# Column mean of 8192x8192: row groups added by VectorE into an accumulator instead of summed one by one by TensorE

## The chip, the cores and the metric

The kernel runs on one core of a Trainium2 chip; the other cores are idle. The metric is the device time of one execution in microseconds (us), as a median over repeated executions. Ratios of two kernels are computed as the mean time of one kernel's runs over that of the other's runs of the same rounds, so they are not quite the ratio of the medians that are quoted beside them. With one core there is one clock to look at: its mean granted value in the profiles is 0.765 before.

## The reference

```python
x = randn(8192, 8192).astype(float32)      # 268.4 MB
out = np.mean(x, axis=0)                    # 8192 numbers
```

Every input number is read once and added once. There is nothing to reuse.

## The kernel before

Rows are taken in groups of 128, one row per partition ("row group"). A group is 4 MiB, a load brings two. TensorE sums over the 128 partitions with a matmul whose weights are all 1/8192, 32 columns wide; four such matmuls sit side by side in the array (the trace shows them overlap: after 613 us a group of four starts every 0.86 us, though it is eight instructions of 0.59 us), and all row groups accumulate in PSUM.

```python
    J = 2
    ld = ctx.enter_context(tc.tile_pool(name="ld", bufs=3))        # 3 x 64 KB per partition
    ...
    for ti in range(n_t - 1):                                       # 31 loads of 8 MiB
        t = ld.tile([P, J, N], f32)
        nc.sync.dma_start(out=t[:], in_=xt[ti])
        for j in range(J):
            sums(t, j, range(NBLK + 1), ti == 0 and j == 0, False)  # 15 matmuls of 512 columns, 4 of 128
    ...                                                             # last 8 MiB in four column pieces:
    cuts = [(0, 8), (8, 12), (12, 15), (15, 16)]                    # blocks of 512 columns
    for lo, hi in cuts:
        for j in range(J):
            sums(t, j, range(lo, hi), False, j == J - 1)
        ...                                                         # VectorE copies the bank, ACT queue sends it
```

## Time and profile before

| | before |
|---|---|
| time, median of 3 | 634.08 us (633.62 to 634.26) |
| span in the profile | 632.0 us |
| load queue, share of 16 DMA engines | 98.4% |
| TensorE (PE) busy | 304.2 us, 48% |
| VectorE (DVE) busy | 3.0 us |

"Busy" is time under instructions of that engine; the shares of different engines overlap. The prediction below shows the lines that say what bounds the kernel. Two more views are needed later. The first is the list of groups of instructions (name, shapes, count, then busy us and mean ns of one, then idle time before them and its cause):

```profile
L47 PE MATMUL bank<-t,ones 128*32 128x512 f32 x1920 | 297.0, 739 | 324.2 <-DMA t<-in_x_dram 324.2
L47 PE MATMUL edge<-t,ones 128*32 128x128 f32 x512 | 51.5, 279 | 0.0
```

The kernel has 1,216 matmuls, but the profile counts 2,432: each fp32 matmul is two instructions here, and each comes with a weight load (2,432 of those too). The second view is the list of transfer queues (packets, megabytes, share of the 16 engines' time):

```profile
q1 hardware_dynamic: 5552, 268.44, 98.4%
q8 instruction: 19, 0.31, 0.2%
q10 hardware_dynamic: 38, 0.03, 0.0%
```

A packet is a piece of a transfer that one DMA engine moves: of the first row's, 3,968 carry 64 KB each in 2.42 us, and 16 at a time at that pace make 433 GB/s, which is the stream's rate. The first row is the loads, the last the results.

### The profile page before, as it was taken

Reading aid. Unit: us, or ns where it says so; the run is one execution under the profiler, and the core shown is the slowest. Engines: PE = TensorE matmul, PEld = TensorE weight load, DVE = VectorE, ACT = ScalarE, POOL = GpSimd, SP = SyncE. Lnnn points to the kernel's source line nnn. Section 1 sums busy time; section 2 is a strip of 40 time slices with the busy share of each in tenths; the row PEclk is TensorE's granted clock in tenths of the full one; section 3 lists DMA queues with packets and bytes.
Section 4 is the critical chain, followed back from the end, with each engine's and each line's share of the span. In section 5 each row is a group of like instructions: output and inputs, shape, how many; then the busy total and the mean of one; then the engine's idle time right before and its main releaser. Section 6 shows DMA issues by size and latency. Waiting matters only on the chain.

```text
span 632.0 us, 4990 instructions
## 1 busy us (share of the span) xinstructions
PE 304.2 (48%) x2432; PEld 99.9 (16%) x2432; DVE 3.0 (0%) x6; POOL 0.2 (0%) x4
## 2 busy tenths in 40 slices
PE   0542555434654345554365534466433655344555
PEld 0210111111211111110111111122101211011111
DVE  0000000000000000000000000000000000000001
POOL 0000000000000000000000000000000000000000
PEclk9977876778776788767777667886678776678769
DMA  9999999999999999999999999999999999999994
GB/s 398 427 437 456 399 465 408 452 411 449 416 444 419 441 444 416 457 402 465 403 456 428 431 428 436 424 448 412 452 423 441 432 431 428 436 431 428 437 401 199
DMA packets 5609, 268.78 MB, mean 425 GB/s; under 512 B 579, under 2 KB 583, under 8 KB 1110
## 3 DMA queue, kind: packets, MB, share of 16 engines
q1 hardware_dynamic: 5552, 268.44, 98.4%
q8 instruction: 19, 0.31, 0.2%
q10 hardware_dynamic: 38, 0.03, 0.0%
HBM read 268.44 MB, written 0.03 MB: 425 GB/s over the span
## 4 chain that ended last, share of the span: by engine, by line
DMA 80%; PE 17%; another core or an unknown queue 2%; SPq 0%; issue 0%; DVE 0%; DVEq 0%
DMA t<-in_x_dram 80%; PE bank L47 15%; PE edge L47 2%; SPq L75 0%; DVE r L83 0%; DVEq L116 0%
## 5 line engine op out<-in xcount | busy, mean ns | idle before, releaser
L47 PE MATMUL bank<-t,ones 128*32 128x512 f32 x1920 | 297.0, 739 | 324.2 <-DMA t<-in_x_dram 324.2
L47 PEld LDWEIGHTS bank<-t,ones 128*32 128x32 f32 x1920 | 85.9, 132 | 489.8 <-DMA t<-in_x_dram 311.7
L47 PE MATMUL edge<-t,ones 128*32 128x128 f32 x512 | 51.5, 279 | 0.0
L47 PEld LDWEIGHTS edge<-t,ones 128*32 128x32 f32 x512 | 23.9, 111 | 38.5 <-issue 38.5
L83 DVE COPY r<-bank 128x512 f32<-128x512 f32 (+1 forms) x4 | 2.8, 690 | 625.1 <-PE bank L47 625.1
L88 DVE COPY redge<-edge 128x128 f32<-128x128 f32 x1 | 0.3, 277 | 0.0
L105 POOL MEMSET const-bfloat16-1.0<- 128x1 bf16 x1 | 0.1, 101 | 0.0
L105 POOL MEMSET const-uint8-127<- 128x1 uint8 x1 | 0.1, 101 | 0.0
L105 POOL MEMSET const-float32-0.0<- 128x1 f32 x1 | 0.1, 98 | 0.2 <-issue 0.2
L105 POOL MEMSET const-float32-1.0<- 128x1 f32 x1 | 0.1, 98 | 0.0
L42 DVE MEMSET ones<- 128x32 f32 x1 | 0.1, 85 | 0.8 <-PEq L105 0.8
## 6 DMA issues: line engine op xcount, KB each, us to landing
t<-in_x_dram SPq DMA_DIRECT2D x1, 4096.0 KB
t<-in_x_dram SPq DMA_DIRECT2D x1, 2048.0 KB, 45.1
t<-in_x_dram SPq DMA_DIRECT2D x1, 1536.0 KB, 48.1
t<-in_x_dram SPq DMA_DIRECT2D x1, 512.0 KB, 39.2
t<-in_x_dram SPq DMA_DIRECT2D x31, 49.0
out_dram<-r ACTq DMA_DIRECT2D x3, 8.0 KB
out_dram<-r ACTq DMA_DIRECT2D x1, 6.0 KB
out_dram<-redge ACTq DMA_DIRECT2D x1, 2.0 KB
```

The costliest lines, as they stand in the source:

```text
L42: nc.vector.memset(ones[:], 1.0 / M)
L47: nc.tensor.matmul(out=dst[32 * q:32 * q + 32, :], lhsT=ones[:], rhs=rhs, start=first, stop=last, tile_position=(0, 32 * q), skip_group_ch ...
L83: nc.vector.tensor_copy(out=r[:32 * n, :], in_=banks[b][:32 * n, :])
L88: nc.vector.tensor_copy(out=r[:], in_=edge[:])
L105: nc = _bacc.Bacc("TRN2", target_bir_lowering=False, num_devices=1)
```

## The change

The intent is to take the arithmetic off TensorE: VectorE adds whole rows into an accumulator of 128x8192, and TensorE only sums over the partitions at the end, for the accumulator and the last two row groups. The accumulator takes 32 KB per partition, so the ring of buffers shrinks from three of 64 KB to two of 64 KB and one of 32 KB. Copies of the results move from VectorE to ACT (ScalarE), except the last small one (`edge`): it stays on VectorE, and its transfer is issued by SP (SyncE) in place of ACT.

```diff
-    ld = ctx.enter_context(tc.tile_pool(name="ld", bufs=3))
+    pairs = ctx.enter_context(tc.tile_pool(name="pairs", bufs=2))
+    singles = ctx.enter_context(tc.tile_pool(name="singles", bufs=1))
+    acc = sg.tile([P, N], f32, name="acc")
 ... (loads go pair, pair, single, pair, pair, single, ...)
-        for j in range(J):
-            sums(t, j, range(NBLK + 1), ti == 0 and j == 0, False)
+        for row in rows:
+            if g == 0:
+                prev = row
+            elif g == 1:
+                nc.vector.tensor_add(out=acc[:], in0=prev, in1=row)
+            elif g < G - 3:
+                nc.vector.tensor_add(out=acc[:], in0=acc[:], in1=row)
+            else:                                   # group 61, in four quarters
+                for c in range(0, N, 4 * F):
+                    s = slice(c, c + 4 * F)
+                    nc.vector.tensor_add(out=acc[:, s], in0=acc[:, s], in1=row[:, s])
 ... (group 62 is loaded whole, group 63 in four column pieces)
+    sums(t[:, 0, :], range(NBLK + 1), True, False)  # group 62
+    for b in range(4):
+        sums(acc, range(4 * b, 4 * b + 4), False, False)
     for lo, hi in cuts:
-        for j in range(J):
-            sums(t, j, range(lo, hi), False, j == J - 1)
+        sums(t[:, 1, :], range(lo, hi), False, True)
 ...
-                nc.vector.tensor_copy(out=r[:32 * n, :], in_=banks[b][:32 * n, :])
+                nc.scalar.copy(out=r[:32 * n, :], in_=banks[b][:32 * n, :])
```

More of the change, by code (lines that the diff above doesn't have):

```diff
@@ L29 @@
     F = 512
-    J = 2
+    W = F // 4
     NBLK = N // F - 1
-    W = F // 4
-    n_t = M // (P * J)
-    xt = x.rearrange("(t p j) c -> t p j c", p=P, j=J)
-    ld = ctx.enter_context(tc.tile_pool(name="ld", bufs=3))
+    G = M // P
+    pairs = ctx.enter_context(tc.tile_pool(name="pairs", bufs=2))
+    singles = ctx.enter_context(tc.tile_pool(name="singles", bufs=1))
     sg = ctx.enter_context(tc.tile_pool(name="sg", bufs=1))
@@ L39 @@
     resp = ctx.enter_context(tc.tile_pool(name="res", bufs=1))
-    ones = sg.tile([P, 32], f32)
-    nc.vector.memset(ones[:], 1.0 / M)
+    acc = sg.tile([P, N], f32, name="acc")
+    ones = sg.tile([P, 32], f32, name="ones")
+    warm = sg.tile([P, 32], f32, name="warm")
+    nc.gpsimd.memset(ones[:], 1.0 / M)
+    nc.scalar.copy(out=warm[:], in_=ones[:])
     banks = [psp.tile([P, F], f32, name=f"bank{b}") for b in range(4)]
@@ L55, in mm, with sums @@
         )
-    def sums(t, j, blocks, first, last):
+    def sums(row, blocks, first, last):
         for i in blocks:
             if i < NBLK:
-                mm(banks[i // 4], i % 4, t[:, j, i * F:(i + 1) * F], first, last)
+                mm(banks[i // 4], i % 4, row[:, i * F:(i + 1) * F], first, last)
             else:
@@ L63, in sums @@
                     c = i * F + q * W
-                    mm(edge, q, t[:, j, c:c + W], first, last)
-    for ti in range(n_t - 1):
-        t = ld.tile([P, J, N], f32)
-        nc.sync.dma_start(out=t[:], in_=xt[ti])
-        for j in range(J):
-            sums(t, j, range(NBLK + 1), ti == 0 and j == 0, False)
-    t = ld.tile([P, J, N], f32)
+                    mm(edge, q, row[:, c:c + W], first, last)
+    g = 0
+    k = 0
+    prev = None
+    while g < G - 2:
+        n = 1 if k % 3 == 2 and g + 2 < G - 2 else 2
+        if n == 2:
+            t = pairs.tile([P, 2, N], f32, name="pair")
+            src = x[g * P:(g + 2) * P, :].rearrange("(p j) c -> p j c", j=2)
+            nc.sync.dma_start(out=t[:], in_=src)
+            rows = [t[:, 0, :], t[:, 1, :]]
+        else:
+            t = singles.tile([P, N], f32, name="single")
+            nc.sync.dma_start(out=t[:], in_=x[g * P:(g + 1) * P, :])
+            rows = [t[:]]
+        for row in rows:
[5 more added lines that the diff above has]
+                nc.vector.tensor_add(out=acc[:], in0=acc[:], in1=row)
+            else:
+                for c in range(0, N, 4 * F):
+                    s = slice(c, c + 4 * F)
+                    nc.vector.tensor_add(out=acc[:, s], in0=acc[:, s], in1=row[:, s])
+            g += 1
+        k += 1
+    t = pairs.tile([P, 2, N], f32, name="pair")
+    nc.sync.dma_start(out=t[:, 0, :], in_=x[g * P:(g + 1) * P, :])
     cuts = [(0, 8), (8, 12), (12, 15), (15, 16)]
     for lo, hi in cuts:
-        nc.sync.dma_start(out=t[:, :, lo * F:hi * F], in_=xt[n_t - 1, :, :, lo * F:hi * F])
+        cs = slice(lo * F, hi * F)
+        nc.sync.dma_start(out=t[:, 1, cs], in_=x[(g + 1) * P:(g + 2) * P, cs])
+    sums(t[:, 0, :], range(NBLK + 1), True, False)
+    for b in range(4):
+        sums(acc, range(4 * b, 4 * b + 4), False, False)
     for lo, hi in cuts:
-        for j in range(J):
-            sums(t, j, range(lo, hi), False, j == J - 1)
+        sums(t[:, 1, :], range(lo, hi), False, True)
         if hi <= NBLK:
@@ L89 @@
             o = out[lo * F:hi * F].rearrange("(q c) -> q c", q=4)
-            nc.scalar.dma_start(out=o, in_=r[0:P:32, :])
+            nc.sync.dma_start(out=o, in_=r[0:P:32, :])
 _INS = ['x']
```

## The prediction

> **What bounds the kernel now.** I read the page of the kernel before from the top: busy shares, slices, queues, chain.
>
> ```profile
> span 632.0 us, 4990 instructions
> PE 304.2 (48%) x2432; PEld 99.9 (16%) x2432; DVE 3.0 (0%) x6; POOL 0.2 (0%) x4
> DMA  9999999999999999999999999999999999999994
> q1 hardware_dynamic: 5552, 268.44, 98.4%
> DMA 80%; PE 17%; another core or an unknown queue 2%; SPq 0%; issue 0%; DVE 0%; DVEq 0%
> ```
>
> PE is busy for half of the span, the load queue for 98.4% of it, and the row of DMA slices has one digit below 9, the last. The chain of waits gives PE 17%, which misleads: it follows PE only to the moment when a buffer comes free. Whether that free buffer was urgent is told by the waits of the queue that issues the loads, and by the issues' time to landing:
>
> ```profile
> SPq L68 <- DMA t<-in_x_dram: 275.3, 28, 20.4
> SPq L68 <- PE edge L47: 270.8, 28, 10.5
> t<-in_x_dram SPq DMA_DIRECT2D x31, 49.0
> ```
>
> Per 8 MiB load the issuer waits 9.8 us for an old load and then 9.7 us for PE to finish that buffer; the new load lands 49.0 us after issue. Carrying 8.39 MB alone takes 19.5 us, so a load stands some 29.5 us behind others in the queue: the PE wait is covered three times over. The windows view says that the transfers themselves are at their pace:
>
> ```profile
> core 0: us, PE busy (x) PEld busy (x) DVE busy (x) POOL busy (x), PEclk, DMA share, GB/s
> 120.00:220.00 100.00, 48.76 (x392) 16.08 (x396) 0.00 (x0) 0.00 (x0) 0.76 1.00 434
> 220.00:320.00 100.00, 50.40 (x396) 16.30 (x391) 0.00 (x0) 0.00 (x0) 0.74 1.00 434
> 420.00:520.00 100.00, 50.63 (x406) 16.47 (x398) 0.00 (x0) 0.00 (x0) 0.74 1.00 433
> ```
>
> All 16 engines are taken all the time (share 1.00) at 433 GB/s. So the time is a head of 2 us, a stream of 268.44 MB, and a tail after the last load. Only the stream's rate, a hole in it, or the tail can change the time.
>
> [...]
>
> **The change part by part.** *Removed:* 62 of 64 row groups from PE. It sat beside the stream, so this is worth nothing by itself.
>
> *Added:* 60 VectorE adds of 128x8192 and four of 128x2048. [...] the sum is 60 x 8.69 + 9.2 = 531 us. One row of 4.19 MB takes 4.19/0.4305 = 9.75 us of the stream, using the mean of mid-run and last-part rates. So VectorE needs 89% of the pace: it becomes the second busiest, not the bound.
>
> *The ring:* 160 KB in place of 192 (the accumulator takes 32), and a pair is held for two adds, 17.4 us, instead of PE's 9.7. Call the buffers A (two rows), B (two), S (one) and let A land at 0. B lands at 19.5, S at 29.3, and A's next load should start then. A is free at 17.5, so 12 us early. B is added from 19.5 to 36.9, and its next load starts at 48.8: again 12 us early. S is added from 36.9 to 45.6, and is wanted at 68.3. An issue costs about 2 us before data (the first load took 21.8 us against 19.5 for its bytes), so the queue never runs dry. Issue to landing should fall from 49 to about 32 us.
>
> *Transfers:* 13 row groups now come in 32 KB runs instead of 64, but the last group cut into small pieces is 4 MiB instead of 8. From the slices near the end, where 8 KB runs moved at about 418 GB/s against 433, I estimate 10 ns lost per run and engine: +0.5 us for the singles, -0.3 for the tail. The stream stays within half a microsecond.
>
> *Head:* pool memset and the ACT warm-up copy run during the first load. 0.
>
> *Tail:* here the change shows. The kernel before ends so:
>
> ```profile
> 607.62 5.15 PE L47 MATMUL bank<-t,ones 128*32 128x512 f32 x27 [10.56 <-DMA t<-in_x_dram]
> 617.41 3.64 PE L47 MATMUL bank<-t,ones 128*32 128x512 f32 x32 [0.34 <-DMA t<-in_x_dram]
> 626.06 1.49 PE L47 MATMUL bank<-t,ones 128*32 128x512 f32 x9 [1.73 <-DMA t<-in_x_dram]
> 628.64 0.28 DVE L88 COPY redge<-edge 128x128 f32<-128x128 f32 x1
> 620.99 8.51 ACTq L85 DMA_DIRECT2D out_dram<-r  x4
> 629.59 0.55 ACTq L90 DMA_DIRECT2D out_dram<-redge  x1
> ```
>
> The next-to-last 8 MiB landed at 607.6; PE was done 21.0 us later, the span 24.4 us later. Weight-load starts in the same view show four 512-column blocks side by side ("a quad") in 0.86 us at full clock and 1.7 at half.
>
> Count the changed kernel from the landing of the last pair that VectorE adds (time 0). The row after it lands at 9.8; the last row's pieces at 14.8, 17.3, 19.1, 19.7. The accumulator's quarters are ready at 8.8 + 2.3k: 11.1, 13.4, 15.7, 18.0. PE starts at 9.9 [...] two quads at 1.7, the rest faster, edge 0.3: done at 15.8. It then has accumulator quarters 1 to 3 (until 18.4), the last one with its edge (19.6), and only then the last row, though most of it has landed: four quads to 23.0, edge to 23.3. That is 2.3 us later than 21.0.
>
> After it, ACT alternates copies and issues in one queue: [...] an issue about 0.6 by the trace (median 628 ns). The first copy starts at 20.4; four copies and three issues put the last issue at about 24.6. Before, the last issue to the end took 632.0 - 629.6 = 2.4 us, so the end is at 27.0 instead of 24.4: **+2.6 us**.
>
> Sum: 634.1 + 0.2 + 2.6, about **637**.
>
> **The rivals.**
> 1. *VectorE becomes the bound.* It needs an add over 9.75 us[...]. Then 61 adds at that duration plus 20 us of head and 27 of tail: at 10.5 us, 690 us. For it: no add of this form is in the trace, each add depends on the one before, and each waits for it by semaphore. Against: [...] a wait of tens of ns in 8.7 us.
> 2. *The shorter ring leaves holes.* For it: cover falls from 30 us to 12, and the 16 engines are not in step: in the last four us before only half were still working (share 0.47), so the fast ones lead by some 4 us. Against: 4 is below 12, and the slow engines, which set each landing, never lack work. If holes came, 1 us in each of 12 rounds would make 649.
> 3. *VectorE's port traffic slows the stream.* One per cent would make 643. [...]
> 4. *The tail costs nothing or gains,* if [...] quarters come quicker: 634 to 635. A gain of more than 2% (below 621.4) would need a stream of 438 GB/s.
>
> **Range and chances.** Tail +1 to +4.5 us and a stream that differs by 0.3% either way give 633 to 641. Faster by over 2%[...]: 0.01. Slower by over 2% (above 646.8) needs rival 1, 2 or a strong 3: 0.05.
>
> **What would show it.** Right: whole-row adds of 8.6 to 8.8 us; VectorE busy 525 to 545 us, waiting for loads at nearly every pair; load queue near 98%, mid-run windows at 431 to 434 GB/s, share 1.00; issue to landing about 32 us; PE busy under 20 us, in the last 18; the last row's matmuls waiting for PE's own order instead of data. Wrong: adds over 9.7 us with loads waiting for VectorE; share below 0.97 in mid-run (rival 2); share 1.00 with GB/s below 428 (rival 3); an end less than 1 or more than 5 us later after the last pair's landing.

The sum came to about 637 us (634.1 + 0.2 + 2.6). Some terms that went into the 2.6, and some of the reasons beside it:

- 8.69 us for a whole-row add and 2.29 us for a quarter. The 531 us of adds, the 89%, the times of the ring and those of the accumulator's quarters rest on these two. No trace had shown them when the forecast was made; the changed kernel's trace shows 8692 and 2287 ns.
- The length of ACT's copies in the tail, and the 692 ns copy of the kernel before. The changed kernel's copies take 587 ns.
- PE's first two quads are taken at 1.7 us. The trace of before has such quads: in its last full burst the granted clock is 0.50 from 607.6 us and quads start 1.7 us apart; from 612 us it is 1.00 and they start 0.86 us apart.
- A faster stream, and one slowed by VectorE. Neither was shown: the stretches above have 433 to 434 GB/s with PE busy half of the time, and VectorE reads no buffer before. The chance of 0.01 is the author's estimate, and the port of rival 3 a guess.

## The result

| | before | changed |
|---|---|---|
| time, median of 4 runs each | 634.11 us (633.62 to 634.26) | 633.14 us (633.02 to 634.28) |
| ratio | | 0.999 (95%: 0.9973 to 1.0007) |
| span in the profile | 632.0 us | 631.2 us |
| PE instructions (matmuls and weight loads) | 4,864 | 228 |
| VectorE busy | 3.0 us | 530.7 us |

The time is the same within 2%, and lies at the lower edge of the range. But the forecast of +2.9 us did not come: the medians differ by -1.0 us, the two traces by -0.8 us. That the time still falls into the range is luck: the low edge stood for a cheap tail and a stream up to 0.3% (1.9 us) shorter, and what came was the full tail and a stream 3.2 us shorter. Here are the lines of the changed kernel's page that answer to those of before: span, busy times, DMA slices, queues and chain.

```profile
span 631.2 us, 470 instructions
PE 12.9 (2%) x114; PEld 4.9 (1%) x114; DVE 530.7 (84%) x65; ACT 3.7 (1%) x6; POOL 0.3 (0%) x5
DMA  9999999999999999999999999999999999999994
q1 hardware_dynamic: 6056, 268.44, 98.6%
q8 instruction: 1, 0.02, 0.0%
DMA 64%; DVE 33%; PE 2%; issue 0%; ACT 0%; ACTq 0%; SPq 0%; DVEq 0%
```

VectorE has taken the place of PE in the chain of waits, for the same harmless reason: it frees the buffers (the queue that issues the loads waits 384.8 us for adds before it sends for pairs, and 91.5 us before singles). The adds have the forecast length, the issues the forecast lead, and the stream its old rate with VectorE running beside it (groups, issues, and one stretch of the windows view, with columns stretch, length, then busy time of PE, PE weight loads, DVE, ACT and POOL, granted clock, DMA share, GB/s):

```profile
L89 DVE TENSOR_TENSOR acc<-acc,pair 128x8192 f32<-128x8192 f32 x47 | 408.5, 8692 | 68.5 <-DMA pair<-in_x_dram 67.8
L89 DVE TENSOR_TENSOR acc<-acc,single 128x8192 f32<-128x8192 f32 x12 | 104.3, 8692 | 0.4
...
single<-in_x_dram SPq DMA_DIRECT2D x12, 4096.0 KB, 31.9
...
pair<-in_x_dram SPq DMA_DIRECT2D x25, 30.9
```

```profile
120.00:220.00 100.00, 0.00 (x0) 0.00 (x0) 90.09 (x11) 0.00 (x0) 0.00 (x0) 1.00 0.99 430
320.00:420.00 100.00, 0.00 (x0) 0.00 (x0) 89.51 (x12) 0.00 (x0) 0.00 (x0) 1.00 1.00 431
```

So where do the 3.7 us between forecast and result lie? The timeline of the last part says it. These are the changed kernel's lines that answer to the tail of before:

```profile
604.44 8.69 DVE L89 TENSOR_TENSOR acc<-acc,pair 128x8192 f32<-128x8192 f32 x1 [2.93 <-DMA pair<-in_x_dram]
...
614.20 4.87 PE L50 MATMUL bank<-pair,ones 128*32 128x512 f32 x27 [614.20 <-DMA pair<-in_x_dram]
...
623.22 3.18 PE L50 MATMUL bank<-pair,ones 128*32 128x512 f32 x26
624.33 0.58 ACT L112 COPY r<-bank 128x512 f32<-128x512 f32 x1 [622.09 <-PE bank L50]
...
627.12 0.29 DVE L117 COPY redge<-edge 128x128 f32<-128x128 f32 x1 [5.06 <-PE bank L50]
627.44 0.66 SPq L119 DMA_DIRECT2D out_dram<-redge  x1
627.88 0.58 ACT L112 COPY r<-bank 96x512 f32<-96x512 f32 x1 [0.71 <-ACT r L112]
628.50 0.74 ACTq L114 DMA_DIRECT2D out_dram<-r  x1
```

From the landing of the same 62 row groups to the end, the kernel before took 632.0 - 607.6 = 24.4 us and the changed one takes 631.2 - 604.4 = 26.8 us: the tail costs 2.4 us, 2.6 were forecast. But the landing itself comes at 604.4 instead of 607.6. **The stream was 3.2 us shorter**, and that step was forecast as +0.2 us. The difference can be seen in the last four microseconds of the loads, before (first) and after:

```profile
622.00:626.00 4.00, 1.92 (x16) 0.42 (x16) 0.69 (x1) 0.00 (x0) 1.00 0.47 185
```

```profile
622.00:626.00 4.00, 4.00 (x47) 1.86 (x46) 0.07 (x1) 0.58 (x1) 0.00 (x0) 1.00 0.19 70
```

Before, half of the DMA engines are still working there; after, most of what is left ends at once. The trace also records when each of the 16 engines reports its part of each load. For the last piece, sorted, in us after the first engine:

```
before   0 0.1 0.1 0.2 0.2 0.2 0.3 0.4 | 3.2 3.2 3.2 3.2 3.3 3.6 | 4.7 4.9
changed  all 16 within 1.0
```

A load has landed when its slowest engine is done: the engines report the last full load of the kernel before between 602.6 and 607.6 us, and PE, idle for it since 597, starts at 607.6. For the last piece, in the kernel before, eight engines are level, six are about 3.2 us behind and two 4.8: steps of about 1.6 us. In its earlier loads the stragglers appear one at a time: at 62.5 us one engine is 1.7 us after the first and the other fifteen are within 0.4.

### The profile page after: what moved, and what is told of

Same layout as the page of the kernel before. It is cut to its first block, busy times and chain, and to the rows that moved or that the text cites. A ratio compares the mean times of both kernels' runs of the same rounds, so it can differ in the third digit from the quotient of the medians.

```text
span 631.2 us, 470 instructions
## 1 busy us (share of the span) xinstructions
PE 12.9 (2%) x114; PEld 4.9 (1%) x114; DVE 530.7 (84%) x65; ACT 3.7 (1%) x6; POOL 0.3 (0%) x5
## 4 chain that ended last, share of the span: by engine, by line
DMA 64%; DVE 33%; PE 2%; issue 0%; ACT 0%; ACTq 0%; SPq 0%; DVEq 0%
DMA pair<-in_x_dram 64%; DVE acc L89 33%; PE bank L50 2%; ACT r L112 0%; ACTq L114 0%; PE edge L50 0%; SPq L77 0%; DVEq L89 0%
## 5 line engine op out<-in xcount | busy, mean ns | idle before, releaser
L89 DVE TENSOR_TENSOR acc<-acc,pair 128x8192 f32<-128x8192 f32 x47 | 408.5, 8692 | 68.5 <-DMA pair<-in_x_dram 67.8
L89 DVE TENSOR_TENSOR acc<-acc,single 128x8192 f32<-128x8192 f32 x12 | 104.3, 8692 | 0.4
L87 DVE TENSOR_TENSOR acc<-pair 128x8192 f32<-128x8192 f32 x1 | 8.7, 8692 | 22.7 <-DMA pair<-in_x_dram 22.7
L50 PE MATMUL bank<-pair,ones 128*32 128x512 f32 x60 | 9.1, 715 | 614.2 <-DMA pair<-in_x_dram 614.2
L93 DVE TENSOR_TENSOR acc<-acc,pair 128x2048 f32<-128x2048 f32 x4 | 8.9, 2287 | 0.0
L50 PEld LDWEIGHTS bank<-pair,ones 128*32 128x32 f32 x60 | 2.8, 127 | 618.7 <-issue 617.9
L112 ACT COPY r<-bank 128x512 f32<-128x512 f32 (+1 forms) x4 | 2.2, 586 | 624.0 <-PE bank L50 623.3
L50 PE MATMUL bank<-acc,ones 128*32 128x512 f32 x30 | 3.8, 595 | 0.0
L50 PE MATMUL edge<-pair,ones 128*32 128x128 f32 x16 | 1.6, 276 | 0.0
L50 PEld LDWEIGHTS bank<-acc,ones 128*32 128x32 f32 x30 | 1.4, 109 | 1.5 <-DVE acc L93 0.7
## 6 DMA issues: line engine op xcount, KB each, us to landing
single<-in_x_dram SPq DMA_DIRECT2D x12, 4096.0 KB, 31.9
pair<-in_x_dram SPq DMA_DIRECT2D x25, 30.9
```

The source lines that it names most:

```text
L50: nc.tensor.matmul(out=dst[32 * q:32 * q + 32, :], lhsT=ones[:], rhs=rhs, start=first, stop=last, tile_position=(0, 32 * q), skip_group_ch ...
L87: nc.vector.tensor_add(out=acc[:], in0=prev, in1=row)
L89: nc.vector.tensor_add(out=acc[:], in0=acc[:], in1=row)
L93: nc.vector.tensor_add(out=acc[:, s], in0=acc[:, s], in1=row[:, s])
L112: nc.scalar.copy(out=r[:32 * n, :], in_=banks[b][:32 * n, :])
```

## The experiments

Three theories could explain a stream that is 3.2 us shorter.

- **Fetch theory.** PE's instructions are themselves fetched by DMA engines that carry the loads, and each fetch holds up the one engine that makes it. The row "instruction" has 19 packets before, for 4,864 PE instructions (256 to a packet), and 1 after, for 228. The packet records before show a fetch of 16,384 bytes taking 1.05 us, and the 64 KB packet that follows it taking 2.92 us on average instead of the usual 2.42; so a fetch costs one engine 1.05 + 0.50 = 1.55 us. Six engines with two fetches and two with three are 18, which is the number of fetches made before the first engines ran out of loads at 622.4 us (the 19th came at 625 us and delayed nothing).
  The trace of the kernel before lets this be counted load by load. In all of its 35 loads, the delays of the 16 engines, in steps of some 1.6 us, add up to the number of fetches that had ended when the load's first engine was done: none in the first two loads, 1 at 62.5 us, 9 at 315.6, 18 from 607.6 on.

  A spread of 4.9 us moves the last landing by only 3.4, because the changed kernel has a spread of 1.0 us too, and because the first engine of the kernel before is done at 622.4 us, 0.5 sooner than that of the changed one (622.9). The 1.0 comes mostly from packets of the same kind on another queue (q14, 8 KB each), which the table below does not count: one came at 394.7 us, and from then on one engine of the changed kernel was 1.1 us late where all had been within 0.7.
- **Ring theory.** Engines drift apart anyway; a shorter ring keeps the fast ones from running ahead.
- **Traffic theory.** PE's reads of all 268 MB of buffers slowed the loads a little.

Each run below was also read from the trace for the landing of the last piece, measured from the run's own first instruction. (The expectations quote 627.4 and 623.8 us for the two kernels; an exact reading gives 627.3 and 623.9.)

| run | fetch packets (q8) | last piece landed | spread of the engines | landing to end | span | time, median | ratio to before |
|---|---|---|---|---|---|---|---|
| before | 19 | 627.3 us | 4.9 us | 4.7 us | 632.0 us | 634.11 us | |
| changed | 1 | 623.9 | 1.0 | 7.3 | 631.2 | 633.14 | 0.9990 |
| e1_fetch | 19 | 627.6 | 4.8 | 7.3 | 634.9 | 636.69 | 1.0043 |
| e2_fetch2 | 37 | 630.8 | 8.3 | 7.4 | 638.2 | 640.58 | 1.0103 |
| e3_ring_pe | 19 | 627.4 | 4.7 | 4.1 | 631.5 | 633.57 | 0.9990 |
| e4_fold | 10 | 625.5 | 2.9 | 6.2 | 631.7 | 633.77 | 0.9994 |
| e5_tail | 1 | 624.5 | 1.8 | 4.2 | 628.7 | 630.35 | 0.9941 |
| e6_tail_fetch | 19 | 627.5 | 4.8 | 4.1 | 631.7 | 633.54 | 0.9990 |
| e7_after_again | 1 | 624.2 | 1.0 | 7.3 | 631.5 | 633.23 | 0.9984 |

All seven gave the right result. The kernel before, run beside them, took 633.98 us (e1 to e4, on one chip) and 634.34 us (e5 to e7, on another). The 95% intervals of the ratios reach at most 0.0016 to either side, so e3, e4 and e6 can't be told from the kernel before by their times.

### e1_fetch: PE's instruction count put back, nothing else

```diff
         for row in rows:
+            for _ in range(19):
+                nc.tensor.matmul(out=spare[0:32, :], lhsT=ones[:], rhs=row[:, 0:8],
+                                 start=True, stop=True, tile_position=(0, 0), ...)
```

> The changed kernel, plus 19 tiny PE matmuls (32x8 results into a spare bank, reading the first 8 columns of the row that just landed) per row group: as many PE instructions as the kernel before had (about 4,900), but no more PE data and the same ring. Fetch theory (the PE instruction stream is itself fetched by the 16 DMA engines, 16 KB at a time, each fetch holding up one engine's share of the loads by some 1.6 us, and a load lands with its slowest engine): 19 to 20 instruction packets in place of 1, the last landing spread over 4.9 us between engines in place of 1.0, the last pair's first add at about 607.6 us instead of 604.4, time about 636.3 us. Ring theory (the shorter ring keeps fast engines from running ahead, so the slow ones end sooner) and traffic theory (PE's large reads of the buffers slowed the loads): nothing changes, first add at 604.4, time 633.1.

Measured: 636.69 us (636.61 to 637.61). The queue and the first add of the last pair read:

```profile
q8 instruction: 19, 0.31, 0.2%
```

```profile
608.05 8.69 DVE L94 TENSOR_TENSOR acc<-acc,pair 128x8192 f32<-128x8192 f32 x1 [2.97 <-DMA pair<-in_x_dram]
```

The landing is back at 608.0 and the spread at 4.8 us, with a ring and VectorE work that are those of the changed kernel, and with almost no data read by PE. The ring and traffic theories expected no change and fall. This kernel has the stream of before and the tail of after, and it takes what the prediction said of the changed kernel (637.0).

### e2_fetch2: twice as many

The same edit with `range(38)`.

> As the run before with 38 tiny matmuls per row group, about 9,650 PE instructions. Fetch theory: 38 packets, five on the most burdened engine in place of three, spread about 8 us, the last pair's first add at about 610 us (604.4 + 3.2 x 5/3), time about 638.5 us. Ring and traffic theories: 604.4 and 633.1.

Measured: 640.58 us (640.02 to 640.89), 37 packets for 9,652 PE instructions, spread 8.3 us, the last pair's first add at 611.3. The spread is that of five fetches on one engine (5 x 1.6 = 8.0); eight engines are level, three some 6.5 us behind and five some 8.2, and 3 x 4 + 5 x 5 is 37. (Here and before, the landings fit eight of the 16 engines taking turns at the fetches; the engines' numbers are not in these records, so which eight they are stays open.) The time is 2 us above what was expected, since I scaled the 3.2 us of before by 5/3. Counted from e1 it is two more fetches on the worst engine, 2 x 1.6 = 3.2 us, and the landing moved from 627.6 to 630.8. PE still waits for loads here, not for instructions:

```profile
PE spare L86 <- DMA pair<-in_x_dram: 342.7, 25, 22.7
```

### e3_ring_pe: the new ring, with PE summing as before

```diff
-            if g == 0: ... elif g == 1: ... tensor_add(...) ...
+            sums(row, range(NBLK + 1), g == 0, False)
 ...
-    for b in range(4):
-        sums(acc, range(4 * b, 4 * b + 4), False, False)
```

> The loads, the ring and the end of the changed kernel, but PE sums every row as in the kernel before; no accumulator, no VectorE adds. Fetch theory: 19 instruction packets, landings spread over 4.9 us at the end, the last piece landed at about 627.4 us as in the kernel before, time about 634. Ring theory: 1 us of spread and the last piece at 623.8 us as in the changed kernel, time about 630.5. The traffic theory agrees with the fetch theory here.

Measured: 633.57 us (633.33 to 633.59); last landing at 627.4 us, spread 4.7. With the short ring and PE's instructions the engines drift exactly as in the kernel before. The ring does nothing here, either way.

### e4_fold: half of PE's instructions, the old ring

```diff
-        for j in range(J):
-            sums(t, j, range(NBLK + 1), ti == 0 and j == 0, False)
+        nc.vector.tensor_add(out=t[:, 0, :], in0=t[:, 0, :], in1=t[:, 1, :])
+        sums(t, 0, range(NBLK + 1), ti == 0, False)
```

> The kernel before with its three 64 KB buffers; VectorE adds the two rows of each pair in place and PE sums the result: half of the PE instructions (about 2,500), same ring, same end, right result. Fetch theory: 10 packets, at most two on one engine, so the last full pair is handed on about 1.6 us earlier (the last piece lands at about 625.8 instead of 627.4), time about 632.5. Ring theory: no change, 634.1. Traffic theory: PE reads half, so also about half of the 3.2 us.

Measured: 633.77 us (633.36 to 634.28), so the expected 632.5 was missed. The cause of the gain was right: 10 packets, and the last piece at 625.5, 1.8 us earlier. The end did not follow, because the fold stands between the last full pair and PE:

```profile
605.88 8.69 DVE L69 TENSOR_TENSOR t<-t 128x8192 f32<-128x8192 f32 x1 [11.64 <-DMA t<-in_x_dram]
614.63 5.49 PE L47 MATMUL bank<-t,ones 128*32 128x512 f32 x27 [14.27 <-DVE t L69]
```

PE starts on that pair at 614.6 instead of 607.6 and reaches the last pieces late: from landing to end it takes 6.2 us instead of 4.7. What the stream gave, the tail took, as in the change itself.

### e5_tail: the changed kernel with the accumulator closed earlier

VectorE stops at group 59. PE sums the accumulator while the last pair is still loading, then groups 60 to 63 as they land.

```diff
-            elif g < G - 3:
+            elif g < G - 4:
                 nc.vector.tensor_add(out=acc[:], in0=acc[:], in1=row)
-            else: ... four quarter adds ...
+            else:
+                if g == G - 4:
+                    sums(acc, range(NBLK + 1), True, False)
+                sums(row, range(NBLK + 1), False, False)
```

> The changed kernel with the accumulator closed two row groups earlier: VectorE adds groups 0 to 59, PE sums the accumulator (before the last pair has landed) and groups 60 to 63 as they land; few PE instructions (about 380). If the explanation stands (fetches gone: last piece lands at 623.8 us; and the 2.4 us of the tail come from PE still holding the accumulator's quarters and the row before when the last row lands), the last piece still lands at 623.8, and the end comes 4.4 us after it, as in e3_ring_pe, instead of 7.4: span about 628.2, time about 630, about 0.6% below the kernel before. If the tail came from the ACT queue's copies and issues instead, the end stays at about 7 us after the landing and the time at 633.

Measured: 630.35 us (630.31 to 630.71). The end comes 4.2 us after the last landing. (The landing is at 624.5, not 623.8: the one fetch that this kernel makes comes at 613.9 us, before its last loads are done; in the changed kernel it comes at 623.6.) PE now has nothing left over and waits for each piece; the timeline shows it idle ahead of the second and the third of the four pieces:

```profile
622.05 1.07 PE L50 MATMUL bank<-pair,ones 128*32 128x512 f32 x8 [0.56 <-DMA pair<-in_x_dram]
...
623.92 1.06 PE L50 MATMUL bank<-pair,ones 128*32 128x512 f32 x6 [0.80 <-DMA pair<-in_x_dram]
```

The copies and issues of ACT are the same in number and length as in the changed kernel (four copies of 0.58 us in both), so the longer tail there was PE's backlog, not ACT's queue. Two parts of that backlog went at once and are not told apart: the accumulator's quarters, and PE's slow start, which in e5 comes at 601 us instead of 614. (In the changed kernel PE's first weight loads, four at a time, follow each other at 0.85 us, and at 0.43 later; over four such steps I count 1.7 us lost. The clock record reads 1.00 there all the same.) This is the fastest version, 0.6% below the kernel before and right in its result.

### e6_tail_fetch: e5 with the tiny matmuls of e1

```diff
+            for _ in range(19 if g < G - 4 else 0):
+                nc.tensor.matmul(out=spare[0:32, :], lhsT=ones[:], rhs=row[:, 0:8], ...)
```

> e5_tail with the 19 tiny matmuls per row group put back (groups 0 to 59), so the instruction fetches return and the tail stays short. Fetch theory, if the two effects simply add: 3.4 us above e5_tail, that is the time of the kernel before within 0.7 us (633.5), with the last piece at about 627.2 and 18 to 20 packets.

Measured: 633.54 us (633.42 to 633.74), last piece at 627.5, 19 packets.

### e7_after_again: the changed kernel in the same rounds

> The changed kernel again, unchanged, to stand on the same chip and in the same rounds as e5_tail and e6_tail_fetch: 633.1, last piece at 623.8, end 7.4 us later.

Measured: 633.23 us (632.91 to 633.62), last piece at 624.2, end 7.3 us later.

e1, e5, e6 and e7 form a square of the two effects:

| median time, us | long tail | short tail |
|---|---|---|
| few PE instructions | 633.23 (e7) | 630.35 (e5) |
| about 4,900 PE instructions | 636.69 (e1) | 633.54 (e6) |

The instructions cost 3.5 and 3.2 us, the tail 2.9 and 3.2: they add up. (e1 is from the other chip's rounds, where the kernel before took 0.4 us less; the ratios give 3.7 for the 3.5.) The kernel before is near the lower right corner, the changed one is the upper left.

## Why the prediction was wrong, point by point

- **What bounds the kernel: right.** The stream of loads and the tail set the time before and after, and the load queue stayed at 98%.
- **VectorE's adds: right.** 8.69 us forecast, 8692 ns measured, each within 1 ns; 531 us in sum forecast, 530.7 busy. Two adds between which no load is awaited are 34 ns apart. Rival 1 fell.
- **The ring: right.** About 32 us from issue to landing were forecast, 30.9 and 31.9 measured; VectorE waits for a load at every pair. Rival 2 fell, by e3 too.
- **Traffic: right.** 430 to 440 GB/s in stretches of 100 us with VectorE 90% busy (431 to 434 were forecast); from 20 to 604 us the mean is 432 in both kernels. Rival 3 fell.
- **The tail: right in mechanism and size.** +2.6 us forecast, 2.4 measured from the landing of the last added pair. e5 shows the cause: without PE's backlog the end comes 3.1 us sooner after the last landing. Rival 4, a tail for nothing, fell.
- **What the removal is worth: wrong, and this is the step that failed.** "*Removed:* 62 of 64 row groups from PE. It sat beside the stream, so this is worth nothing by itself." PE's time did sit beside the stream. Its instructions did not: they came over DMA engines that carry the loads. The term forecast as 0 measured -3.2 us at the landing, and 3.2 to 3.5 us in the two pairs of runs that add or remove only these instructions. With it the sum would have been 634.1 - 3.2 + 2.6 = 633.5 (the -3.2 is the whole stream, so the +0.2 for transfers is in it); 633.14 was measured.

Two lines could have given it away. The queue list had 19 instruction packets, which I passed over, because 0.2% of the engines' time is 20 us of one engine, or 1.25 us if shared by 16. But it isn't shared evenly: three fetches on one engine are 4.8 us, and the slowest engine sets the landing. And the share of 0.47 in the last four microseconds stands in the prediction, read as engines "not in step" with a harmless lead. The right question was why half of them were behind, and by whose work.

## What to carry to other kernels

In a kernel bound by a stream of loads, look for anything else that uses the DMA engines, the instruction stream included, and charge it to the slowest engine and not to the mean (here three fetches, 4.8 us, and not 1.25); the sign here was a DMA share of 0.47 in the last four microseconds of the loads. Some 4,900 small unrolled instructions on an engine with time to spare lengthened the stream here by 3.2 to 3.5 us. Close an accumulation early enough that the engine that finishes the job has no backlog when the last piece lands: here that was worth about as much as the instructions, and only both together brought a gain well clear of the noise (0.6%).
